# An encoder layer on one core: the score unit moves from the bias tables into the split factors of queries and keys, and four tiles are loaded at an earlier place in the code

## The chip, the core and the metric

The kernel runs on one core of a Trainium2 chip. A core has a matrix engine (TensorE, PE in the profile; PEld is its loading of weights), a vector engine (VectorE, DVE), a scalar engine (ScalarE, ACT), a general engine (GpSimd, POOL) and a queue engine (SyncE, SP), which in this kernel issues every DMA. Each engine runs its own list of instructions in order and waits on semaphores for the others. The metric is the device time of one execution in microseconds (us), lower is better.

## The reference

One layer of a bidirectional encoder with width 1024 is applied to two inputs with the same weights: a prompt of 512 positions and a sample of 1024 positions. The kernel treats them as three chunks of 512 positions: chunk 0 is the short sequence (the prompt), chunks 1 and 2 are the long one (the sample).

```python
def encoder_layer(x, ...):
    h = rmsnorm(x, n_pre)
    aq, ak, av, gq, gk, gv, gr, glr = split(h @ w_in)
    o_attn = dilated_attention(heads(aq), heads(ak), heads(av))   # 8 heads of 64
    o_gla = gla_mixer(gq, gk, gv, gr, glr, ...)                   # gated linear attention
    x = x + rmsnorm(concat([o_attn, o_gla]) @ w_out, n_post)
    h = rmsnorm(x, n_ffn_pre)
    a, g = split(h @ w_up)
    f = (gelu(dwconv_centred(a, conv_w, conv_b)) * g) @ w_down
    return x + rmsnorm(f, n_ffn_post)

# in each of the three branches of dilated_attention:
    s = einsum('bnqrhd,bnkrhd->bnrhqk', qb, kn) * (Dh ** -0.5)
    s = where(valid, s - slopes * dist, NEG)
```

The three branches (windows of 128, 512 and 2048 positions at strides 1, 4 and 16) are merged by their softmax denominators. The kernel computes them as one softmax: the penalties, the masks and how many branches see a key are in one table for each head, `nbias`, which is an input made on the host.

## The kernel before

**Numbers in two halves.** Every float32 operand of the large matrix products is split into a high and a low half of 16 bits (or of a shortened float32), and a product is three matmuls: high by high, high by low, low by high (`mm3`, lines 353 to 355). To use the range of 16 bits, each group of weight columns is scaled by a power of two that is measured on the chip. The class `Group` does that: `measure` squares the weights on ACT (L253), `finish` sums on PE (L260) and DVE (L261), makes the power on POOL (L367, L368) and DVE (L216), and stores in `undo` the factor that takes a product back to its true unit (L220, L265). The twelve blocks of 128 columns that hold queries and keys of both kinds of attention belong to six groups, `G_FM[0]` to `G_FM[5]`; the first four hold the attention's queries and keys, and each of these holds those of two heads.

**Queries and keys.** `store_fm` takes a finished projection block out of PSUM, splits it (`split_psum`: ACT L358 for the high half, DVE L363 for the low) and stores it in DRAM. Before the change queries are multiplied by the constant -2^-15 there and keys by 2^-15, whatever the group's scale, so that their products are in a unit of the group's own. That unit is kept in `Group.scores`: column 0 is the factor that turns a product into a true score (undo squared, over 8, times 2^30), column 1 its reciprocal.

**Attention.** `attention(seq)` goes through 8 heads, and in each through tiles of 128 queries: 8 tiles for the long sequence, 4 for the short. Tiles with more than 512 keys are done in two pieces, which makes 14 steps a head for the long sequence. A step's work is spread over the next eleven in a pipeline: `scores` (PE, L593 and L594, into a PSUM bank), `reduce` (DVE, L608: product times factor plus table, with a running minimum), `expo` (ACT, L620), `part_hi` (DVE L627 and POOL L628 for the reciprocal of the denominator, `rs`; ACT L631 for the high half of the probabilities `p`), `part_lo` (DVE, L638), `turn` (a transposing DMA from `p` to `pt`, L647), `pv` (PE, L674) and `out` (ACT, DVE, and a DMA to the mix in DRAM, L689). POOL also starts each tile with a copy of one column (L602).

The table of a head is `bias`: 128 rows by 1664 columns for the long sequence, 1152 for the short one. `load` brings it in (L559). Because the products are in the group's own unit, the table has to be brought to that unit too: it is multiplied on POOL by column 1 of `scores` in slices of 128 columns (L565), 13 slices a head for the long sequence and 9 for the short, 176 in all. The slices are queued in `tables`; those of the first two heads are done ahead of the pipeline, the others at up to two a step. Two heads' tables are held at a time: the table of head h+2 is loaded when head h has left its buffer.

**What runs beside what.** `_weave` alternates the steps of a main piece of work with those of a side piece. The long attention is woven into the input projection of chunks 1 and 2 (`main2`). Then `main3` (the projection of chunk 0 and half of the output projection of chunks 1 and 2, `outproj_early`) is woven with the linear attention of the long sequence. The rest of the output projection follows, then the MLP of chunks 1 and 2 with the short sequence's attention and linear attention beside it, and at last the MLP of chunk 0. `outproj_early` multiplies the first half of the mixed features (four tiles `mix`, loaded by `load_mix`, L961) by the output weights. The pool `early`, which holds these tiles, has four buffers for them.

**The order of the instructions.** The code is traced once, and a planner decides when the kernel is built in which order each engine and each queue gets its instructions. It goes by its own estimate of the times: among the instructions of an engine that are ready by that estimate it takes the one that the code has first. So the order on an engine is near that of the code but not the same, and a DMA can stand long before the place at which the code asks for it.

Of the kernel before, what the change touches and what calls it, by code (L numbers as in the profile page):

```python
# [7 lines left out]
F32 = mybir.dt.float32  # L8
# [5 lines left out]
ALU = mybir.AluOpType  # L14
# [156 lines left out]
def encoder(ctx, tc, xp, xs, n_pre, w_in, wg, g_gla, w_out, n_post, n_ffn_pre, w_up, conv, w_down,  # L171
# [51 lines left out]
    class Rows:  # L223
# [3 lines left out]
        def __init__(self, nm):  # L227
            self.scale = const.tile([128, 1], F32, name=f"rows_{nm}")
# [8 lines left out]
    class Group:  # L237
# [1 line left out]

        def __init__(self, nm, n, rows, *more, scores=False):
            self.n, self.rows, self.more, self.at = n, rows, more, 0

            self.scores = const.tile([128, 2], F32, name=f"scores_{nm}") if scores else None
            self.scale = const.tile([128, 1], F32, name=f"up_{nm}")
            self.undo = const.tile([128, 1 + len(more)], F32, name=f"undo_{nm}")

# [9 lines left out]
        def finish(self):  # L258
            ps, total = bank(), small()
            nc.tensor.matmul(ps[:, 0:self.n], ones, self.sums[:, 0:self.n], start=True, stop=True)  # L260
            nc.vector.tensor_reduce(out=total, in_=ps[:, 0:self.n], axis=mybir.AxisListType.X, op=ALU.add)  # L261
            power_of_two(self.scale, total, 1.0)
            u = self.undo[:, 0:1]
            times(u, self.scale, self.rows.scale)
            nc.vector.reciprocal(out=u, in_=u)  # L265
            for i, x in enumerate(self.more):
                if x is not None:
                    times(self.undo[:, 1 + i:2 + i], u, x)
            if self.scores is not None:
                c = [self.scores[:, i:i + 1] for i in range(2)]  # L270
                nc.gpsimd.tensor_scalar(out=c[0], in0=u, scalar1=u, scalar2=PART ** -2 / 8.0, op0=ALU.mult, op1=ALU.mult)
                nc.vector.reciprocal(out=c[1], in_=c[0])

    r_pre, r_fpre = Rows("pre"), Rows("fpre")

# [13 lines left out]
        + [O_GQ, O_GQ + 128, O_GK, O_GK + 128]  # L289
    FM_ORDER = [0, 4, 1, 5, 2, 6, 3, 7, 8, 9, 10, 11]  # L290
    TM = [(O_V, 256), (O_V + 256, 256), (O_GV, 256), (O_GV + 256, 256), (O_GR, 256), (O_GR + 256, 272)]
    G_FM = [Group(f"fm{i}", 4, r_pre, scores=i < 4) for i in range(6)]
    G_TM = [Group(f"tm{i}", 4, r_pre, (1.0 / PART / P_SCALE, None, 0.5)[i // 2]) for i in range(6)]
    G_UP = [Group(f"up{b}", 4, r_fpre, 0.5) for b in range(NFB)]
    GROUPS = [range(i, i + 3) for i in range(0, 18, 3)] + [range(18, 22)]
# [138 lines left out]
    def store_fm(c, i, ps):  # L434
        seq, o0 = where(c)
        m = FM_ORDER[i]
        if m < 8:
            t = tmp.tile([128, 2, CH], FP16, name="stq", tag="two")
            split_psum(ps, t[:, 0], t[:, 1], -PART if m < 4 else PART)
            nc.sync.dma_start(out=QK[seq][m][:, :, o0:o0 + CH].rearrange("s p t -> p s t"), in_=t)  # L440
            stored.add((c, m))
        else:
            o = stage.tile([128, CH], F32, name="sto", tag="sto", bufs=3)
            nc.scalar.activation(out=o, in_=ps, func=ACTF.Copy, scale=G_FM[i // 2].undo[:, 0:1])
            nc.sync.dma_start(out=GQK[seq][m - 8][:, o0:o0 + CH], in_=o)
# [99 lines left out]
    def attention(seq):  # L545
# [6 lines left out]
        with ExitStack() as es:  # L552
            hp = es.enter_context(tc.tile_pool(name=f"ah{seq}", bufs=nbuf, side="right", reuse_waits="tile"))
            up = es.enter_context(tc.tile_pool(name=f"au{seq}", bufs=2, side="right", reuse_waits="tile"))
            heads, vs, st, pts, pvs, tables = {}, {}, {}, {}, {}, []

            def load(h):
                bias = hp.tile([128, bw], F32, name="bias", tag="bias")
                nc.sync.dma_start(out=bias, in_=nbias[h, :, 0:bw])  # L559
                qs = hp.tile([128, T], FP16, name="qs", tag="qs")  # L560
                kk = hp.tile([128, 2, T], FP16, name="kk", tag="kk")
                unit = G_FM[h // 2].scores[:, 1:2]

                def scale(c0, c1):
                    nc.gpsimd.tensor_scalar(out=bias[:, c0:c1], in0=bias[:, c0:c1], scalar1=unit, scalar2=3e38,  # L565
                                            op0=ALU.mult, op1=ALU.min)
                tables.extend(lambda c0=c0: scale(c0, min(c0 + 128, bw)) for c0 in range(0, bw, 128))
                r = slice(h % 2 * DH, (h % 2 + 1) * DH)
                nc.sync.dma_start(out=qs, in_=QK[seq][h // 2][:, r, :])
                for s in range(2):  # L570
                    nc.sync.dma_start(out=kk[s * DH:(s + 1) * DH],
                                      in_=QK[seq][4 + h // 2][:, r, :].rearrange("s p t -> p s t"))
                heads[h] = (bias, qs, kk)
# [23 lines left out]
            def reduce(h, qt, k0, k1, last):  # L597
                bias = heads[h][0]
                miss = ph_sb[:, seq * 32 + h * nkt + qt:seq * 32 + h * nkt + qt + 1]
                if k0 == first[qt]:  # L600
                    st[h, qt] = up.tile([128, T + 1], F32, name="t", tag="t", bufs=1 + nh)
                    nc.gpsimd.tensor_copy(out=st[h, qt][:, T:T + 1], in_=miss)  # L602
                    st["m"] = miss
                t = st[h, qt]
                ps = st.pop((h, qt, k0))
                for a, b, col in bias_ranges(qt, k0, k1):
                    m = up.tile([128, 1], F32, name="m", tag="m", bufs=8)
                    nc.vector.tensor_tensor_reduce(  # L608
                        out=t[:, a:b], in0=ps[:, a - k0:b - k0], in1=bias[:, col:col + b - a],
                        scale=G_FM[h // 2].scores[:, 0:1],  # L610
                        scalar=st["m"], op0=ALU.add, op1=ALU.min, accum_out=m)
                    st["m"] = m
                if last:
                    st[h, qt] = (t, m)
# [84 lines left out]
            for h in range(nbuf):  # L699
                load(h)  # L700
                load_v(h)
                while tables:
                    tables.pop(0)()
            yield True
            stages = [(1, reduce, "piece"), (2, expo, "tile"), (3, part_hi, "tile"), (4, part_lo, "tile"),
                      (5, turn, "tile"), (9, pv, "pair"), (11, out, "pair")]
# [1 line left out]
            for i in range(len(steps) + 12):  # L708
                for lag, fn, kind in reversed(stages):
                    if not 0 <= i - lag < len(steps):  # L710
                        continue
                    x = steps[i - lag]
                    if kind == "piece":
                        fn(*x)
                    elif x[4] and kind == "tile":
                        fn(x[0], x[1])
                    elif x[4] and x[1] % 2:
                        fn(x[0], x[1] // 2)
                if i < len(steps):
                    scores(*steps[i])  # L720
                for _ in range(-(-bw // 128 * HEADS // len(steps)) + 1):
                    if tables:
                        tables.pop(0)()
                if i - 1 in ends:
                    h = ends[i - 1]
                    while not {(c, m) for c in cs for m in (h // 2, 4 + h // 2)} <= stored:
                        yield None
                    load(h)
                if i - 9 in ends:
                    load_v(ends[i - 9])  # L730
                yield True
# [225 lines left out]
    def load_mix(c, pool, bufs, ks=range(NK)):  # L957

        for k in ks:
            t = pool.tile([128, 2, CH], F32R, name="mix", tag="mix", bufs=bufs)  # L960
            nc.sync.dma_start(out=t.bitcast(F32), in_=MX[c][:, k * 128:(k + 1) * 128, :].rearrange("s p t -> p s t"))  # L961
            yield t
# [32 lines left out]
        for t in range(4):  # L995
            mm3(ps[t], tuple(m[:, s, t * 128:(t + 1) * 128] for s in range(2)), (wh[:, 0, :], wl[:, 0, :]), first, last)

    def outproj_early(c, pool):

        mix = list(load_mix(c, pool, 4, range(4)))  # L1000
        for half in range(2):
            ps = [bank(dense) for _ in range(4)]
            for k, m in enumerate(mix):
                outproj_step(ps, m, k == 0, k == 3)
                yield True
            for t in range(4):
                o = pool.tile([128, 512], F32, name="yp", tag="yp", bufs=2)
                nc.scalar.activation(out=o, in_=ps[t], func=ACTF.Copy)
                nc.sync.dma_start(out=rows(YP[c], t)[:, half * 512:(half + 1) * 512], in_=o)
# [150 lines left out]
    with ExitStack() as es:  # L1160
# [43 lines left out]
        def main3():  # L1204
            yield from inproj_fm([(0, h0[0])], range(12))
            yield from inproj_tm([(0, h0[0])], (4, 5))
            for c in (1, 2):
                yield from outproj_early(c, early)
        with tc.tile_pool(name="early", bufs=1, side="right", reuse_waits="tile") as early:
            _weave(main3(), linear(1), 46, 188)  # L1210
        act2 = ctx.enter_context(tc.tile_pool(name="act2", bufs=1, side="right", reuse_waits="tile"))
        mx = es.enter_context(tc.tile_pool(name="mx", bufs=1, side="right", reuse_waits="tile"))
# [129 lines left out]
```

## Time and profile before

| | us |
|---|---|
| median of 3 runs | 2166.89 (2157.13 to 2170.65) |
| the profiled execution, its own time | 2164.9 |
| its span | 2163.1 |
| mean granted PE clock, share of full speed | 0.94 |
| long attention beside the projection, about | 138 to 491 |
| linear attention of the long sequence, early output projection, about | 500 to 786 |
| short attention beside the MLP, about | 905 to 1170 |

All times in the profile are us from the span's start unless marked ns. In the slices of the page the span is cut into 40 equal parts of 54 us, and each digit is a busy share in tenths; the row PEclk is the clock that PE was granted. A line of a group names the source line, the engine, the operation, output and inputs with shapes, the count, and then busy time in us, the mean of one in ns, the idle time of the engine just before these instructions and what ended most of it. In a row of waits stand the engine, what it waited to do, what ended the wait, the total in us, how often, and the longest. In a timeline stand start, length, engine, line and instruction, and in brackets the idle time before it with what ended it; in the merged rows of a timeline, x13 is thirteen instructions of one kind.

### The profile page before, as it was taken

To read this page: it belongs to the slowest core of one execution; us is meant where nothing else is said; L and a number is where in the kernel's file an instruction comes from. 1 tells how busy PE (TensorE), PEld (TensorE's weight loads), DVE (VectorE), ACT (ScalarE), POOL (GpSimd) and SP (SyncE) were. 2 spreads that over 40 slices of the span, in tenths; PEclk is the share of its full clock that TensorE was granted. 3 is DMA by queue.
4 is the path that set the end of the run, shared out by engine and by line. 5 is a ranking of instruction groups with operands and counts; after the bars stand their busy time and mean duration, and the time that the engine had idled before them with its cause. 6 is when DMAs were issued, how large, how long until landed. Compare 5 with 4: busy or idle time off the path is not lost. (4 is left out here: it accounts for less than half of the span.)

```text
span 2163.1 us, 31915 instructions
## 1 busy us (share of the span) xinstructions
PE 1914.6 (89%) x11960; PEld 1199.5 (55%) x11960; DVE 1203.2 (56%) x2383; ACT 974.8 (45%) x1858; POOL 355.9 (16%) x697
## 2 busy tenths in 40 slices
PE   3797776888888958898898999999999998999997
PEld 3664334665457737744545564656564774565554
DVE  4256544575544426756466555465555378566666
ACT  5256545565524214645655453343333264433343
POOL 3303243331011002343321000010100031000001
PEclk8898887899999879999899999999999999999998
DMA  6468988987534466844544131222140466333331
GB/s 199 114 137 181 160 169 152 157 168 213 176 114 153 157 230 213 245 99 105 124 99 95 45 98 59 59 77 70 40 156 25 150 229 209 107 103 102 93 103 49
DMA packets 393118, 283.14 MB, mean 131 GB/s; under 512 B 174306, under 2 KB 342498, under 8 KB 392964
## 3 DMA queue, kind: packets, MB, share of 16 engines
q1 hardware_dynamic: 392964, 281.11, 48.2%
q8 instruction: 94, 1.54, 0.3%
q14 instruction: 60, 0.49, 0.1%
HBM read 196.02 MB, written 51.48 MB: 114 GB/s over the span
## 5 line engine op out<-in xcount | busy, mean ns | idle before, releaser
L353 PE MATMUL bank<-c,w_hi 128*128 128x512 f16 x704 | 267.0, 379 | 0.0
L354 PE MATMUL bank<-c,w_hi 128*128 128x512 f16 x704 | 266.8, 379 | 0.0
L355 PE MATMUL bank<-c,w_lo 128*128 128x512 f16 x704 | 266.8, 379 | 0.0
L353 PEld LDWEIGHTS <-w_hi 128*128 128x128 f16 x1376 | 138.3, 100 | 167.9 <-issue 21.9
L355 PEld LDWEIGHTS <-w_lo 128*128 128x128 f16 x1376 | 136.8, 99 | 166.8 <-issue 9.4
L354 PEld LDWEIGHTS <-w_hi 128*128 128x128 f16 x1376 | 137.4, 100 | 151.1 <-issue 8.5
L111 ACT ACTIVATE w_hi<-w_raw,up_up 128x512 f16<-128x512 f32 x176 | 125.8, 718 | 188.6 <-PE bank L354 101.3
L120 DVE SCALAR_TENSOR_TENSOR w_lo<-w_raw,up_up,w_hi 128x512 f16<-128x512 f32 x176 | 131.1, 747 | 98.1 <-PE bank L355 42.8
L111 ACT ACTIVATE w_hi<-w_raw 128x512 fp32r<-128x512 f32 x144 | 90.5, 629 | 209.4 <-PE bank L355 172.5
L353 PE MATMUL bank<-b,w_hi 128*128 128x512 f16 (+1 forms) x464 | 175.0, 378 | 6.4 <-DVE ya L1065 6.4
L355 PE MATMUL bank<-b,w_lo 128*128 128x512 f16 (+1 forms) x464 | 174.8, 377 | 5.1 <-DVE w_lo L120 5.1
L354 PE MATMUL bank<-b,w_hi 128*128 128x512 f16 (+1 forms) x464 | 175.0, 377 | 1.1 <-DVE b L363 1.1
L638 DVE SCALAR_TENSOR_TENSOR p<-t,rs,p 128x512 f16<-128x512 f32 (+2 forms) x96 | 89.9, 942 | 146.3 <-ACT p L631 145.6
L353 PE MATMUL bank<-w_hi,fh 128*128 128x512 f32 x352 | 143.1, 411 | 17.9 <-DVE ya L1099 13.9
L118 DVE TENSOR_TENSOR w_lo<-w_raw,w_hi 128x512 fp32r<-128x512 f32 x144 | 98.6, 689 | 99.2 <-PE bank L354 75.5
L1065 DVE SCALAR_TENSOR_TENSOR ya<-bank,cvt,ya 128x511 f32<-128x511 f32 x176 | 107.4, 614 | 62.5 <-ACT ya L1067 58.6
L354 PE MATMUL bank<-w_lo,fh 128*128 128x512 f32 x352 | 139.6, 397 | 0.8 <-DVE w_lo L118 0.8
L355 PE MATMUL bank<-w_hi,fl 128*128 128x512 f32 x352 | 139.6, 397 | 0.0
L631 ACT ACTIVATE p<-t,rs 128x512 f16<-128x512 f32 (+2 forms) x96 | 81.6, 859 | 127.0 <-POOL rs L628 117.1
L565 POOL TENSOR_SCALAR bias<-bias,scores_fm 128x128 f32<-128x128 f32 x176 | 127.7, 749 | 65.5 <-DMA bias<-in_nbias_dram 65.2
L253 ACT ACTIVATE w_junk<-w_raw 128x512 bf16<-128x512 f32 (+1 forms) x136 | 85.4, 628 | 114.6 <-DMA w_raw<-in_w_up_dram 69.8
L1135 DVE TENSOR_TENSOR y<-bank,y 128x512 f32<-128x512 f32 x144 | 97.4, 687 | 55.9 <-PE bank L355 55.3
(193 smaller groups left out, 4048.2 us busy)
## 6 DMA issues: line engine op xcount, KB each, us to landing
w_raw<-in_w_up_dram SPq DMA_DIRECT2D x88, 512.0 KB
w_raw<-in_w_in_dram SPq DMA_DIRECT2D x44, 512.0 KB
w_raw<-in_w_down_dram SPq DMA_DIRECT2D x36, 512.0 KB
mix<-mx SPq DMA_DIRECT2D x24, 512.0 KB
xin<-x SPq DMA_DIRECT2D x20, 512.0 KB
xin<-in_x_sample_dram SPq DMA_DIRECT2D x16, 512.0 KB
w_raw<-in_w_out_dram SPq DMA_DIRECT2D x32, 256.0 KB
bias<-in_nbias_dram SPq DMA_DIRECT2D x8, 832.0 KB
```

The costliest lines, as they stand in the source:

```text
L111: self.nc.scalar.activation(out=self.hi[i], in_=raw, func=ACTF.Copy, scale=1.0 if group is None else group.scale)
L118: self.nc.vector.tensor_tensor(out=lo, in0=raw, in1=hi.bitcast(F32), op=ALU.subtract)
L120: self.nc.vector.scalar_tensor_tensor(out=lo, in0=raw, scalar=group.scale, in1=hi, op0=ALU.mult, op1=ALU.subtract)
L253: nc.scalar.activation(out=junk[:, :raw.shape[1]], in_=raw, func=ACTF.Square, accum_out=self.sums[:, self.at:self.at + 1])
L353: nc.tensor.matmul(out, ah, bh, start=start, stop=False)
L354: nc.tensor.matmul(out, ah, bl, start=False, stop=False)
L355: nc.tensor.matmul(out, al, bh, start=False, stop=stop)
L565: nc.gpsimd.tensor_scalar(out=bias[:, c0:c1], in0=bias[:, c0:c1], scalar1=unit, scalar2=3e38, op0=ALU.mult, op1=ALU.min)
L631: nc.scalar.activation(out=p[:, 0:n], in_=t[:, kf:T], func=ACTF.Copy, scale=rs)
L638: nc.vector.scalar_tensor_tensor(out=p[:, n:2 * n], in0=t[:, kf:T], scalar=rs, in1=p[:, 0:n], op0=ALU.mult, op1=ALU.subtract)
L1065: nc.vector.scalar_tensor_tensor(out=out, in0=src, scalar=cw[:, j:j + 1], in1=out, op0=ALU.mult, op1=ALU.add)
L1135: nc.vector.tensor_tensor(out=y[t][:, cols], in0=ps[t], in1=y[t][:, cols], op=ALU.add)
```

## The change

The unit of the products goes into the factors with which queries and keys are split. With u the group's `undo` and P = 2^-15, keys are multiplied by min(u, P) and queries by -max(u / P, 1) u / 8. The product of the two is -u^2 / 8 in either case, so that the products of the score matmuls are true scores with the sign turned, and the table is used as it was loaded. `Group.heads` holds the two factors, made on POOL in `finish`; the queue of slices and its places in `attention` are gone, and the reduction multiplies by 1.0.

```diff
-            if self.scores is not None:
-                c = [self.scores[:, i:i + 1] for i in range(2)]
-                nc.gpsimd.tensor_scalar(out=c[0], in0=u, scalar1=u, scalar2=PART ** -2 / 8.0, op0=ALU.mult, op1=ALU.mult)
-                nc.vector.reciprocal(out=c[1], in_=c[0])
+            if self.heads is not None:
+                k, q = (self.heads[:, i:i + 1] for i in range(2))
+                nc.gpsimd.tensor_scalar(out=k, in0=u, scalar1=PART, scalar2=None, op0=ALU.min)
+                nc.gpsimd.tensor_scalar(out=q, in0=u, scalar1=1.0 / PART, scalar2=1.0, op0=ALU.mult, op1=ALU.max)
+                nc.gpsimd.tensor_scalar(out=q, in0=q, scalar1=u, scalar2=-0.125, op0=ALU.mult, op1=ALU.mult)
...
             t = tmp.tile([128, 2, CH], FP16, name="stq", tag="two")
-            split_psum(ps, t[:, 0], t[:, 1], -PART if m < 4 else PART)
+            f = G_FM[i // 2].heads
+            split_psum(ps, t[:, 0], t[:, 1], f[:, 1:2] if m < 4 else f[:, 0:1])
...
                 kk = hp.tile([128, 2, T], FP16, name="kk", tag="kk")
-                unit = G_FM[h // 2].scores[:, 1:2]
-
-                def scale(c0, c1):
-                    nc.gpsimd.tensor_scalar(out=bias[:, c0:c1], in0=bias[:, c0:c1], scalar1=unit, scalar2=3e38,
-                                            op0=ALU.mult, op1=ALU.min)
-                tables.extend(lambda c0=c0: scale(c0, min(c0 + 128, bw)) for c0 in range(0, bw, 128))
...
-                        out=t[:, a:b], in0=ps[:, a - k0:b - k0], in1=bias[:, col:col + b - a],
-                        scale=G_FM[h // 2].scores[:, 0:1],
+                        out=t[:, a:b], in0=ps[:, a - k0:b - k0], in1=bias[:, col:col + b - a], scale=1.0,
...
                 load_v(h)
-                while tables:
-                    tables.pop(0)()
...
                     scores(*steps[i])
-                for _ in range(-(-bw // 128 * HEADS // len(steps)) + 1):
-                    if tables:
-                        tables.pop(0)()
```

The second part moves the loading of the four `mix` tiles of chunk 1 from the start of its early output projection to a place ahead of `main3` and of the linear attention. The tiles of chunk 2 are loaded where they were.

```diff
-    def outproj_early(c, pool):
-
-        mix = list(load_mix(c, pool, 4, range(4)))
+    def outproj_early(c, pool, mix):
+
...
-            for c in (1, 2):
-                yield from outproj_early(c, early)
+            yield from outproj_early(1, early, mix)
+            yield from outproj_early(2, early, list(load_mix(2, early, 4, range(4))))
         with tc.tile_pool(name="early", bufs=1, side="right", reuse_waits="tile") as early:
+            mix = list(load_mix(1, early, 4, range(4)))
             _weave(main3(), linear(1), 46, 188)
```

More of the change, by code (lines that the diff above doesn't have):

```diff
@@ L237, in encoder, with __init__ @@
     class Group:
-        def __init__(self, nm, n, rows, *more, scores=False):
+        def __init__(self, nm, n, rows, *more, heads=False):
             self.n, self.rows, self.more, self.at = n, rows, more, 0
-            self.scores = const.tile([128, 2], F32, name=f"scores_{nm}") if scores else None
+            self.heads = const.tile([128, 2], F32, name=f"heads_{nm}") if heads else None
             self.scale = const.tile([128, 1], F32, name=f"up_{nm}")
@@ L291, in encoder @@
     TM = [(O_V, 256), (O_V + 256, 256), (O_GV, 256), (O_GV + 256, 256), (O_GR, 256), (O_GR + 256, 272)]
-    G_FM = [Group(f"fm{i}", 4, r_pre, scores=i < 4) for i in range(6)]
+    G_FM = [Group(f"fm{i}", 4, r_pre, heads=i < 4) for i in range(6)]
     G_TM = [Group(f"tm{i}", 4, r_pre, (1.0 / PART / P_SCALE, None, 0.5)[i // 2]) for i in range(6)]
@@ L554, in attention @@
             up = es.enter_context(tc.tile_pool(name=f"au{seq}", bufs=2, side="right", reuse_waits="tile"))
-            heads, vs, st, pts, pvs, tables = {}, {}, {}, {}, {}, []
+            heads, vs, st, pts, pvs = {}, {}, {}, {}, {}
             def load(h):
```

## The prediction, before the result was known

> **What bounds the kernel now.** I read the page first: busy shares, then the 40 slices.
>
> ```profile
> span 2163.1 us, 31915 instructions
> PE 1914.6 (89%) x11960; PEld 1199.5 (55%) x11960; DVE 1203.2 (56%) x2383; ACT 974.8 (45%) x1858; POOL 355.9 (16%) x697
> PE   3797776888888958898898999999999998999997
> PEclk8898887899999879999899999999999999999998
> L565 POOL TENSOR_SCALAR bias<-bias,scores_fm 128x128 f32<-128x128 f32 x176 | 127.7, 749 | 65.5 <-DMA bias<-in_nbias_dram 65.2
> ```
>
> TensorE (PE) is the bound: the second half of the slices is nearly full at full clock. What can be gained lies in the first half, where both the busy share and the granted clock (PEclk) are low. POOL is busy only 16%, but a third of that is the scaling that the change removes, and its 65.2 us of waiting for the table's DMA stand on an engine that runs in order. So the next view was who waits for whom, from 138 to 500 us, where the long sequence's attention runs beside its input projection.
>
> ```profile
> PE bank L593 <- DVE m L608: 48.4, 16, 9.7
> PE bank L674 <- issue: 18.1, 4, 6.1
> DVE p L638 <- ACT p L631: 106.5, 37, 15.1
> ACT p L631 <- POOL rs L628: 93.7, 29, 15.1
> POOL bias L565 <- DMA bias<-in_nbias_dram: 47.5, 6, 9.3
> ```
>
> Columns: total us, times, longest. Read upwards it is one chain: POOL waits for a table, ACT's p waits for POOL's rs, DVE's second half of p waits for ACT, and PE's score matmul (L593) waits for a PSUM bank that DVE's reduce (L608) frees. The timeline of the four engines and of SP around one of the six table loads shows it:
>
> ```profile
> 212.06 0.54 SPq L559 DMA_DIRECT2D bias<-in_nbias_dram  x1
> 213.59 0.64 POOL L602 COPY t<-ph_sb 128x1 f32<-128x1 f32 x1 [1.37 <-DVE p L638]
> 223.54 9.04 POOL L565 TENSOR_SCALAR bias<-bias,scores_fm 128x128 f32<-128x128 f32 x13 [9.31 <-DMA bias<-in_nbias_dram]
> 232.67 0.23 POOL L628 TENSOR_SCALAR rs<-rs 128x1 f32<-128x1 f32 x1
> 218.95 0.07 DVE L608 DVE_READ_ACCUMULATOR2_ANT m<- 128x1 f32 x1
> 232.93 1.15 ACT L631 ACTIVATE p<-t,rs 128x1024 f16<-128x1024 f32 x1 [15.14 <-POOL rs L628]
> 234.11 1.28 DVE L638 SCALAR_TENSOR_TENSOR p<-t,rs,p 128x1024 f16<-128x1024 f32 x1 [15.09 <-ACT p L631]
> 225.90 2.16 PE L674 MATMUL bank<-pt,v 128*128 128x256 f16 x12 [3.96 <-issue]
> 238.00 0.53 PE L593 MATMUL bank<-kk,qs 128*128 128x448 f16 x1 [3.49 <-DVE m L608]
> ```
>
> POOL does no other work from 214.2 to 232.67: 9.31 us of waiting and 13 slices in 9.04 us, about 18 us. The two small operations of the softmax (L628, L602) stand behind it, and DVE and ACT do nothing for 15 us. PE holds out on projection work for a while, then waits. Six heads have this; the last two, during which no further table is loaded, have none. Stage by stage:
>
> ```profile
> 142.00:423.00 281.00, 217.16 (x1225) 125.20 (x1223) 157.25 (x391) 152.74 (x280) 91.45 (x195) 0.86 0.86 165
> 423.00:491.00 68.00, 57.20 (x469) 46.27 (x468) 52.27 (x113) 48.30 (x83) 19.80 (x45) 0.94 0.77 161
> 461.00:491.00 30.00, 27.56 (x238) 22.80 (x237) 25.32 (x53) 21.70 (x37) 9.13 (x17) 1.00 0.83 172
> 237.00:249.00 12.00, 6.95 (x24) 3.34 (x24) 10.30 (x26) 9.58 (x20) 1.80 (x6) 0.50 0.91 189
> 408.00:424.00 16.00, 9.93 (x66) 7.10 (x65) 3.39 (x11) 1.28 (x3) 9.27 (x14) 0.80 1.13 137
> 905.00:1085.00 180.00, 156.36 (x760) 88.79 (x759) 98.52 (x230) 100.05 (x204) 75.21 (x140) 0.93 0.50 117
> 1085.00:1125.00 40.00, 40.00 (x207) 19.87 (x205) 24.52 (x57) 20.90 (x38) 12.09 (x24) 1.00 0.43 101
> ```
>
> Columns: stretch, length, busy us of PE, PEld, DVE, ACT, POOL, then granted clock, DMA share and GB/s. I use busy PE times clock as the work done, in us at full clock. The row from 237 shows the second half of a stall's price: after it, PE ran 12 us at a clock of 0.50.
>
> **The change part by part.** The sum is made against the profiled execution: 2164.9 us, of which 2163.1 are span; that is 2.0 below the median of 2166.89.
>
> *The slices in the long attention (104, of which 78 lie inside six heads).* They go, with the wait in front. In the first row (heads 0 to 5 with the six blocks) PE did 217.16 x 0.86 = 187 us of work in 281. Without blocks the same work takes 187 over the share of the time that PE then works. From rows: the last two heads reach 57.20 x 0.94 / 68 = 0.79, but their first part still recovers from the block that ends at 423; the last head alone reaches 27.56 x 1.00 / 30 = 0.92, but it has no loads of tables, queries or keys beside it. At 0.79 the stretch takes 237 us (44 less), at 0.92 203 (78 less). I take the middle, 0.85: 220 us, **61 less**. What is late next: the vector engines, busy 157 us of these 281 on DVE, would be at 157/220 = 71%, which they bear (25.32 of 30 in the last head); and the DMA, a rival below. The table itself is now waited for by L608 on DVE, behind which DVE's weight splits and banks would queue; it is issued when the head two before has finished, so it has about one head (over 30 us) for the 11.5 us from 212.06 to 223.54. I count that wait at nothing; the rival prices it.
>
> *The slices in the short attention (72), beside the MLP.*
>
> ```profile
> ACT p L631 <- POOL rs L628: 23.4, 7, 9.5
> 955.75 6.29 POOL L565 TENSOR_SCALAR bias<-bias,scores_fm 128x128 f32<-128x128 f32 x9 [4.76 <-DMA bias<-in_nbias_dram]
> 968.52 0.58 PE L353 MATMUL bank<-b,w_hi 128*128 128x512 f16 x1 [4.47 <-DVE ya L1065]
> ```
>
> The first row is the wait from 905 to 1125. The block is shorter (11 us) and PE has more other work, but DVE's convolution (L1065) then comes late. From 905 to 1085 PE did 156.36 x 0.93 = 145 us in 180: 35 lost. Not all comes from the blocks (a group's end stalls too, when the down projection needs its last column blocks), and the block at 1101 lies in a stretch of 40 us without loss. Between 0 and 35 I take half, **17 less**.
>
> *The first 26 slices.*
>
> ```profile
> 58.27 3.48 POOL L565 TENSOR_SCALAR bias<-bias,scores_fm 128x128 f32<-128x128 f32 x5
> 62.71 1.28 DVE L408 SCALAR_TENSOR_TENSOR xin<-xin,small,g 128x1024 f32<-128x1024 f32 x1 [6.64 <-POOL small L368]
> 64.14 1.09 PE L415 MATMUL bank<-idt,xin 128*128 128x128 f32 x4 [6.67 <-DVE xin L408]
> ```
>
> They hold back the row scale of the last input tile, and with it DVE and PE, by up to 6.6 us. What follows there waits for weights from memory, so between 0 and 6.6 I take **3 less**.
>
> *The score unit.* Four groups lose one POOL operation and one reciprocal on DVE and get three POOL operations; each group's are done before its first store, some beside the norms:
>
> ```profile
> L271 POOL TENSOR_SCALAR scores_fm<-undo_fm x4: 265/266/267, 14.4 to 156.9; 128x1 f32<-128x1 f32 x4
> L358 ACT ACTIVATE stq<-bank x24: 573/578/658, 49.6 to 596.3; 128x512 f16<-128x512 f32 x24
> L358 ACT ACTIVATE a<-bank,rows_pre x16: 672/687/714, 18.1 to 522.7; 128x512 f16<-128x512 f32 x16
> L363 DVE SCALAR_TENSOR_TENSOR stq<-bank,stq x24: 672/688/693, 52.3 to 600.8; 128x512 f16<-128x512 f32 x24
> L363 DVE SCALAR_TENSOR_TENSOR a<-bank,rows_pre,a x16: 740/743/751, 21.2 to 523.4; 128x512 f16<-128x512 f32 x16
> ```
>
> Eight more on POOL at 0.27 us are 2.1 us, of which 0.5 stand ahead of the first norms: **1 more**, between 0 and 2. The 24 stores of queries and keys now take their factor from a tile. The nearest operation that does so (into a) costs 0.11 us more on ACT and 0.055 on DVE: 2.6 and 1.3 us, hidden beside PE's projection; with that cover gone, 4 us. The other way, 176 reductions (L608) take 1.0 instead of a tile's factor; by the same 0.055 DVE gains up to 9.7 us, or nothing. It isn't PE's time; I count nothing.
>
> *The mix tiles.* The order on each queue is made by a planner when the kernel is built, not by the code, and there the tiles are early already:
>
> ```profile
> 504.11 0.66 SPq L961 DMA_DIRECT2D mix<-mx  x1
> 517.44 1.52 SPq L961 DMA_DIRECT2D mix<-mx  x3
> L353 PE MATMUL bank<-w_hi,mix x192: 387/393/797, 690.6 to 1734.7; 128*128 128x512 f32 x192
> ```
>
> PE first reads them at 690.6, over 170 us after their issue. Moved up, they are the same four DMAs of about 0.5 us of SP, at most 2 us ahead of the gates' loads and a weight load, with PE still on projection work: nothing, between 0 and 2.
>
> Sum: 61 + 17 + 3 - 1 = 80 less: 2164.9 - 80 = **2085**.
>
> **The rivals.** *Full gain.* PE works at the last head's 0.92 through the long attention (78), nearly all the short one's loss goes (30) and the start gives 5: 113 less, 2052. For it: the vector engines have room. Against it: the last head has no loads beside it. One page speaks for it: the Trainium skill, "DMA: Bandwidth & Descriptors", Latency and other measured facts, puts a transposing DMA at 261 GB/s, so that DMA should not be what limits here; the trace's 137 GB/s from 408 to 424, where transposes share the queue with a table, does not reach that.
>
> *DMA becomes the bound.* DMA share times 281 us is 0.86 x 281 = 242; if the engines can't hold more than one, the stretch shrinks by 39 at most, and by 13 if no more than 0.9. For it: 1.13 at only 137 GB/s, and PE's value matmuls (L674) waiting 18.1 us with no compute engine late, just after transposes behind a table. Against it: a share over one means that packets' times include queueing. With 26 for the stretch, 10 for the short one and 3 at the start less 1: 38 less, 2127.
>
> *The wait moves to DVE, and the kernel is slower.* If the planner now issues a table late, DVE's reduce stops in order with everything behind it. Today a block costs POOL 18 us a head. A wait of the 8 us that POOL now waits (47.5/6) leaves some gain, about 2130. From 18 us a head on it turns to a loss; at 25 us, 6 x 7 = 42 more, 2207. Against it: the load's place in the code and the buffers that let it start are the same.
>
> *It does nothing for PE* (other work hides the blocks): 2165. Against it: the 48.4 us and the clock of 0.50.
>
> **How the numbers follow.** Forecast (2062 to 2110) 0.52; full gain 0.18; DMA 0.18; wait on DVE with some gain 0.05, with a loss 0.03; nothing 0.04. About 1% is what a measurement of this kernel can tell from no change. Faster by more (below 2145): 0.52 + 0.18 + 0.18 + 0.04 = 0.92, where the wait with some gain counts 0.04; within 1%: 0.05; slower: 0.03. The range takes in the forecast, the DMA case and most of the full gain: 2045 to 2132.
>
> **What would show it.** Right: no POOL line of 9 us in the attention, ACT's wait for rs below 20 us from over 90, heads of some 37 us where they took 47, a clock near 0.95 from 142 on, PE's bank waits on L608 below 20. Wrong: waits of DVE's L608 for the table's DMA, value matmuls waiting longer for their transposes, or a clock still at 0.86. The stretch from 1200 on should only shift. What would break the forecast most easily is another order of the queues: the planner sees different times on POOL and may place everything else anew.

## The result, and the profile after

| | before | after |
|---|---|---|
| median of the runs on the same chip, us | 2162.77 (2157.13 to 2170.65) | 2094.15 (2091.49 to 2099.08) |
| the profiled execution's span, us | 2163.1 | 2097.3 |
| mean granted PE clock | 0.94 | 0.954 |

The ratio is 0.9683, with a 95% interval from 0.9642 to 0.9723: 68.6 us less. The forecast was 2085 with a range of 2045 to 2132, so the time came out 9 us above the forecast and inside the range.

These lines of the page of after answer to the first fence of the prediction: span, busy shares, PE's slices and clock. The table's slices (L565) have no successor; the last line is now the group that computes the high half of `p`.

```profile
span 2097.3 us, 31743 instructions
PE 1898.3 (91%) x11960; PEld 1194.8 (57%) x11960; DVE 1194.5 (57%) x2379; ACT 976.5 (47%) x1858; POOL 235.4 (11%) x529
PE   3898888798999958999999999999999979999997
PEclk8998989998899979999999999999999989999998
L627 ACT ACTIVATE p<-t,rs 128x512 f16<-128x512 f32 (+2 forms) x96 | 81.4, 858 | 74.6 <-DMA pt<-p 54.6
```

POOL has 120 us less work. Line numbers have moved by three or four: scores are L590 and L591, reduce is L605, `rs` on POOL L624, `p` on ACT L627 and on DVE L634, the transposing DMA L643, the value matmuls L670. What the last line says is new: ACT, before it may write `p`, waits 54.6 us for old transposes (the DMA from `p` to `pt`) that still read the buffer.

To say where the time went, the stages need markers that exist in both kernels. The first and last `rs` on POOL serve; these rows give count, durations in ns, and first and last start, for the long sequence (x64) and the short one (x32), first of before, then of after.

```profile
L628 POOL TENSOR_SCALAR rs<-rs x64: 203/209/1171, 141.9 to 488.9; 128x1 f32<-128x1 f32 x64
L628 POOL TENSOR_SCALAR rs<-rs x32: 208/220/759, 930.7 to 1155.0; 128x1 f32<-128x1 f32 x32
```

```profile
L624 POOL TENSOR_SCALAR rs<-rs x64: 207/208/1302, 133.2 to 448.1; 128x1 f32<-128x1 f32 x64
L624 POOL TENSOR_SCALAR rs<-rs x32: 207/208/758, 890.5 to 1085.1; 128x1 f32<-128x1 f32 x32
```

| stage, us | before | after | difference | forecast |
|---|---|---|---|---|
| start to the first `rs` | 141.9 | 133.2 | -8.7 | -3, and 1 for the unit |
| long attention | 347.0 | 314.9 | -32.1 | -61 |
| from there to the short attention | 441.8 | 442.4 | +0.6 | 0 |
| short attention | 224.3 | 194.6 | -29.7 | -17 |
| from there to the end of the span | 1008.1 | 1012.2 | +4.1 | 0 |

Together that is 65.8 less, against a forecast of 80. The last row is spread between runs: the same kernel, run again (below), took 1004.5 there. So the sum came out near, but the two large terms did not: the long attention gave half of its forecast, the short one nearly twice.

The waits of after in the long attention (130 to 460 us), to be set beside those of before from 138 to 500:

```profile
PE bank L590 <- DVE m L605: 21.2, 10, 3.8
PE bank L670 <- issue: 16.2, 3, 6.8
PE bank L670 <- DMA pt<-p: 8.4, 3, 3.2
DVE p L634 <- ACT p L627: 78.7, 40, 9.3
ACT p L627 <- DMA pt<-p: 48.3, 7, 9.3
ACT p L627 <- POOL rs L624: 15.4, 18, 2.7
```

The old chain is gone: ACT's wait for `rs` fell from 93.7 us (longest 15.1) to 15.4 (longest 2.7), and POOL waits for no table. But DVE still waits 78.7 us for ACT's `p`, where it was 106.5, and the reason is the row above the last: ACT waits 48.3 us, seven times, for transposes. Before, that row, and the one of the value matmuls, were these:

```profile
ACT p L631 <- DMA pt<-p: 2.8, 1, 2.8
PE bank L674 <- DMA pt<-p: 2.6, 2, 2.2
```

The timeline of after shows one of the seven waits, first SP's queue and then the engines:

```profile
202.47 0.58 SPq L562 DMA_DIRECT2D bias<-in_nbias_dram  x1
203.10 0.58 SPq L568 DMA_DIRECT2D kk<-qk  x1
203.78 12.28 SPq L643 DMA_TRANSPOSE pt<-p  x3
216.15 0.54 SPq L92 DMA_DIRECT2D w_raw<-in_w_in_dram  x1
```

```profile
216.04 1.15 ACT L627 ACTIVATE p<-t,rs 128x1024 f16<-128x1024 f32 x1 [5.65 <-DMA pt<-p]
217.23 1.28 DVE L634 SCALAR_TENSOR_TENSOR p<-t,rs,p 128x1024 f16<-128x1024 f32 x1 [6.29 <-ACT p L627]
215.99 1.38 PE L670 MATMUL bank<-pt,v 128*128 128x256 f16 x12 [2.53 <-DMA pt<-p]
```

A table and the keys' second half are issued, and the three transposes behind them, those of the last three tiles of a head, keep SP for 12.28 us. `p` has three buffers; ACT wants the next, its old transpose has not read it, and DVE waits for ACT. PE's value matmuls wait for the same transposes. The table's load, which had delayed `rs` by way of POOL, is now one of the transfers ahead of them; how much of the delay is its own, the experiments have to show. Rows by stretch (length, busy us of PE, PEld, DVE, ACT and POOL, granted clock, DMA share, GB/s) put the two kernels side by side. First come the long and the short attention of before, then the long attention of after, its part up to the end of the sixth table's wait at 382 us (the prediction cut before at 423 us, likewise at the end of the sixth block), the rest of it, and its short attention:

```profile
142.00:489.00 347.00, 272.36 (x1675) 169.77 (x1673) 207.78 (x502) 199.44 (x360) 110.73 (x239) 0.87 0.85 164
931.00:1155.00 224.00, 200.41 (x937) 106.25 (x935) 134.27 (x315) 125.03 (x252) 70.51 (x140) 0.95 0.47 103
```

```profile
133.00:449.00 316.00, 267.23 (x1683) 168.85 (x1681) 202.57 (x502) 201.32 (x362) 58.82 (x163) 0.92 0.96 180
133.00:382.00 249.00, 208.08 (x1210) 120.97 (x1207) 153.03 (x391) 154.00 (x280) 37.52 (x120) 0.92 0.99 182
382.00:449.00 67.00, 59.15 (x473) 47.88 (x474) 49.55 (x111) 47.32 (x82) 21.30 (x43) 0.92 0.82 176
890.00:1085.00 195.00, 189.79 (x921) 102.82 (x920) 131.76 (x315) 125.35 (x253) 32.31 (x86) 0.99 0.51 115
```

In the long attention the DMA engines' share rose from 0.85 to 0.96, and to 0.99 up to 382 us. Share times length hardly changed: 0.85 x 347 = 295 us before, 0.96 x 316 = 303 after. In the short attention, at a share of 0.51, PE is now busy 189.79 of 195 us at a clock of 0.99, where it was 200.41 of 224 at 0.95.

### The profile page after: what moved, and what is told of

It reads as the page before. It is cut to its first block, busy times and chain, and to the rows that moved or that the text cites. A ratio compares the mean times of both kernels' runs of the same rounds, so it can differ in the third digit from the quotient of the medians.

```text
span 2097.3 us, 31743 instructions
## 1 busy us (share of the span) xinstructions
PE 1898.3 (91%) x11960; PEld 1194.8 (57%) x11960; DVE 1194.5 (57%) x2379; ACT 976.5 (47%) x1858; POOL 235.4 (11%) x529
## 5 line engine op out<-in xcount | busy, mean ns | idle before, releaser
L356 PE MATMUL bank<-b,w_hi 128*128 128x512 f16 (+1 forms) x464 | 172.4, 372 | 1.0 <-DVE b L365 1.0
L355 PE MATMUL bank<-b,w_hi 128*128 128x512 f16 (+1 forms) x464 | 172.5, 372 | 0.0
L634 DVE SCALAR_TENSOR_TENSOR p<-t,rs,p 128x512 f16<-128x512 f32 (+2 forms) x96 | 89.7, 943 | 94.6 <-ACT p L627 94.2
L254 ACT ACTIVATE w_junk<-w_raw 128x512 bf16<-128x512 f32 (+1 forms) x136 | 85.5, 628 | 121.2 <-DMA w_raw<-in_w_up_dram 74.8
L627 ACT ACTIVATE p<-t,rs 128x512 f16<-128x512 f32 (+2 forms) x96 | 81.4, 858 | 74.6 <-DMA pt<-p 54.6
L355 PE MATMUL bank<-w_hi,a 128*128 128x256 f16 (+1 forms) x384 | 108.9, 285 | 7.4 <-DVE v2t L365 6.7
```

The lines of the kernel that those rows point to most:

```text
L254: nc.scalar.activation(out=junk[:, :raw.shape[1]], in_=raw, func=ACTF.Square, accum_out=self.sums[:, self.at:self.at + 1])
L355: nc.tensor.matmul(out, ah, bh, start=start, stop=False)
L356: nc.tensor.matmul(out, ah, bl, start=False, stop=False)
L627: nc.scalar.activation(out=p[:, 0:n], in_=t[:, kf:T], func=ACTF.Copy, scale=rs)
L634: nc.vector.scalar_tensor_tensor(out=p[:, n:2 * n], in0=t[:, kf:T], scalar=rs, in1=p[:, 0:n], op0=ALU.mult, op1=ALU.subtract)
```

## The experiments

The theory after the result had two parts. First, the whole gain comes from POOL's slices, which no longer stand in front of `rs`; the moved tiles add nothing. Second, the long attention gave only half because the DMA engines became its limit. The rivals: that the load moved early contributes; that the wait for the table's DMA, not the slices' own time, was the cost; that something else (a buffer too few, the queue by which the table is issued) holds the long attention.

### One part of the change at a time

Before with one line taken out, so that the tables are used as they were loaded, in another unit than the products (the penalties in its result are wrong, the other work is the same); before with the moved tiles alone; and the change without the moved tiles.

```diff
-                tables.extend(lambda c0=c0: scale(c0, min(c0 + 128, bw)) for c0 in range(0, bw, 128))
```

> The kernel before, with the slices left out and nothing else changed: the tables are not brought to the unit of the products, so the attention is computed with wrong penalties. If the slices on POOL in front of the softmax's small operations are the whole cause, it gains what the change gained, 60 to 75 us (2088 to 2103). If the cheaper reduction (606 against 666 ns on DVE, 176 times, 10 us in all) or the new order of the stores carries a part, it gains only 40 to 55 us.

```diff
-    def outproj_early(c, pool):
+    def outproj_early(c, pool, mix):
...
-            for c in (1, 2):
-                yield from outproj_early(c, early)
+            yield from outproj_early(1, early, mix)
+            yield from outproj_early(2, early, list(load_mix(2, early, 4, range(4))))
...
+            mix = list(load_mix(1, early, 4, range(4)))
```

> The kernel before with only the four mix tiles loaded at the earlier place. By my theory nothing: within 4 us of before, since the tiles were issued 170 us ahead of their use already. By the rival (they free the queue of DMAs later on, or hold it up) 5 us or more either way.

For the third the same edit was taken back in the changed kernel.

> The change without its second part: the score unit in the split factors, the mix tiles loaded at the old place. By my theory the same as the whole change, 2094 within 5 us. By the rival, 5 us or more behind it.

| kernel | median, us | ratio to before, 95% interval |
|---|---|---|
| before without the slices | 2086.3 | 0.9648 [0.9624, 0.9673] |
| before with the moved tiles | 2162.12 | 0.9999 [0.998, 1.0019] |
| the change without the moved tiles | 2091.72 | 0.967 [0.9649, 0.9691] |

The slices, with the wait for their table, are the whole gain, and the moved tiles nothing. Taking the slices out costs a line and gives 76 us; the changed kernel, which also pays for the unit in the split factors, gives 71 without the moved tiles. The two intervals overlap, so the unit's own price, some 5 us at most by the medians, is not told from nothing. The new wait is there without any other edit; from the waits of before without the slices, 130 to 460 us:

```profile
ACT p L630 <- DMA pt<-p: 45.1, 7, 9.3
ACT p L630 <- POOL rs L627: 13.6, 22, 1.8
```

One rival is left: that the slices slow DVE down while both work in the same memory. The records show no sign of it. The 80 pieces of the reduction that aren't the first of their tile took 523/676/810 ns (min/median/max) in before, and 523/676/812 ns with the slices taken out.

### The slices kept, but not in front of `rs` while the table is on its way

Before, with the slices of the long sequence held back for five steps, so that the table has landed, and then done a step at a time; a small operation on DVE makes their factor, so that they can't be moved ahead of that step.

```diff
+            held, HOLD = [0], 5 if nh == 2 else 0
...
-                for _ in range(-(-bw // 128 * HEADS // len(steps)) + 1):
-                    if tables:
-                        tables.pop(0)()
+                held[0] -= 1
+                if tables and held[0] < 0:
+                    gate = up.tile([128, 1], F32, name="gate", tag="gate", bufs=4)
+                    nc.vector.tensor_scalar(out=gate, in0=st["m"], scalar1=0.0, scalar2=tables[0][0], op0=ALU.mult, op1=ALU.add)
+                    for _ in range(-(-bw // 128 * HEADS // len(steps)) + 1):
+                        if tables:
+                            tables.pop(0)[1](gate)
```

> The kernel before with all 176 slices, but those of a later head held back: in the long attention they start five steps after the table was asked for, in the short one with the next step, up to two (four) a step, and each step's slices wait for that step's reduction through a small DVE operation. POOL does the same work but no longer waits for a table with the small operations behind it. If the in-order wait on POOL is the cause, most of the gain is there: 2095 to 2120. If POOL's work itself or its use of memory beside DVE is the cause, it stays near before, 2145 to 2170.

Measured: 2136.2, ratio 0.9879 [0.9856, 0.9901], 26 us less than before on that chip and short of what was expected. Its waits from 130 to 460 us:

```profile
ACT p L633 <- POOL rs L630: 46.5, 35, 3.8
ACT p L633 <- DMA pt<-p: 40.4, 6, 9.1
POOL bias L566 <- DVE gate L726: 17.7, 14, 2.5
```

The longest wait for `rs` fell from 15.1 to 3.8 us, so the table is no longer waited for; but 46.5 us are left in 35 pieces, and the transposes are waited for as in the changed kernel. So with the table's wait gone, a third of what leaving the slices out gives is there. Slices of 0.7 us still stand in front of an `rs` of 0.2 us, but the experiment also adds a wait of its own: in the last row POOL waits 17.7 us for the small operation on DVE, again with `rs` behind it. How much of the rest is the slices' own time stays open. By the markers, the long attention gained 11 us (336.1) and the short one, whose slices also came step by step, 18 (206.6).

### The long sequence alone

The change, with slices, unit and factor of the short sequence as they were before.

```diff
...
-            split_psum(ps, t[:, 0], t[:, 1], f[:, 1:2] if m < 4 else f[:, 0:1])
+            if seq:
+                split_psum(ps, t[:, 0], t[:, 1], f[:, 1:2] if m < 4 else f[:, 0:1])
+            else:
+                split_psum(ps, t[:, 0], t[:, 1], -PART if m < 4 else PART)
...
+                if not seq:
+                    tables.extend(lambda c0=c0: scale(c0, min(c0 + 128, bw)) for c0 in range(0, bw, 128))
...
+                        scale=1.0 if seq else G_FM[h // 2].scores[:, 0:1],
...
```

> The changed kernel, but with the short sequence as before: constant factors, tables brought to the products' unit by the 72 slices beside the MLP. The profiles of before and after put 29 us of the gain between the start of the short attention and its end, so by that reading this is 25 to 30 us slower than the changed kernel (2117 to 2124). By my prediction's sizes (61 long, 17 short) it is 17 slower, 2110.

Measured: 2125.83, ratio 0.9832 [0.9801, 0.9862]. Before stood at 2161.58 on this chip, so the long sequence and the start are worth 36 us, and the other 32 of the change's 68 are the short sequence's. Its short attention, by the same marker, is back at 223.5 us, where the changed kernel has 194.6:

```profile
L639 POOL TENSOR_SCALAR rs<-rs x32: 207/222/758, 887.7 to 1111.2; 128x1 f32<-128x1 f32 x32
```

### What limits the long attention now

Seven runs on the changed kernel. A fourth buffer for `p` (paid for with one buffer each of `sto` and `stg`, the staging tiles of the projection's stores); the tables issued by ACT; only the tables of heads 0 and 1 loaded, and used by the later heads too; only the high half of `p` transposed, and read twice by the value matmuls; the last two together; and the changed kernel itself, with the fourth buffer again beside it. The third, fourth and fifth leave transfers out but no work of PE, DVE or ACT.

```diff
...
-                p = up.tile([128, 2 * T], FP16, name="p", tag="p", bufs=3)
+                p = up.tile([128, 2 * T], FP16, name="p", tag="p", bufs=4)
...
```

> The changed kernel with four buffers instead of three for the probabilities p; the space comes from one buffer each of the two staging tiles of the projection's stores (2 instead of 3). In the changed kernel ACT waits 48 us for old transposes to leave p. If this wait is what holds the heads at 41 us, most of it goes and the kernel gains 10 to 25 us (2070 to 2084). If the transposes themselves are too slow behind the table's load, the wait moves on to PE's value matmuls and nothing is gained, 2090 to 2098.

```diff
-                nc.sync.dma_start(out=bias, in_=nbias[h, :, 0:bw])
+                nc.scalar.dma_start(out=bias, in_=nbias[h, :, 0:bw])
```

> The changed kernel with the tables' loads issued from ACT instead of SP, so that they stand in another queue than the transposes. If the transposes are late because they stand behind the table in one queue, ACT's wait for p falls below 20 us and the kernel gains 10 to 20 us. If both share the same DMA engines' time, nothing changes but 16 issues on ACT: 2090 to 2100.

```diff
-                bias = hp.tile([128, bw], F32, name="bias", tag="bias")
-                nc.sync.dma_start(out=bias, in_=nbias[h, :, 0:bw])
+                bias = heads[h - 2][0] if h >= 2 else hp.tile([128, bw], F32, name="bias", tag="bias")
+                if h < 2:
+                    nc.sync.dma_start(out=bias, in_=nbias[h, :, 0:bw])
```

> The changed kernel with only the first two heads' tables loaded in each sequence; the later heads use them again, so their penalties are wrong. 8.4 MB of loads less. If the table's load is what delays the transposes, ACT's wait for p nearly goes and the kernel gains 15 to 30 us (2065 to 2080). If the transposes are slow by themselves, it gains less than 8 us.

```diff
-                nc.sync.dma_start_transpose(out=pts[h, qt // 2][:, 0:2 * nb, o:o + 128],
-                                            in_=st.pop((h, qt))[:, 0:2 * nb * 128])
+                nc.sync.dma_start_transpose(out=pts[h, qt // 2][:, 0:nb, o:o + 128],
+                                            in_=st.pop((h, qt))[:, 0:nb * 128])
...
-                        nc.tensor.matmul(ps[:, :n], v[:, kt, :], turned(pt, qp, j, kt, n), start=i + j == 0,
+                        nc.tensor.matmul(ps[:, :n], v[:, kt, :], turned(pt, qp, 0, kt, n), start=i + j == 0,
```

> The changed kernel with only the high half of the probabilities transposed; the value matmuls read the high half twice, so the result loses its low half while PE's work stays the same. The transposes move half the bytes (12.8 MB less in the long attention). If DMA time is what now bounds the long attention, ACT's wait for p and PE's wait for pt nearly go and the kernel gains more than leaving out the tables did: 25 to 40 us (2055 to 2070). If the vector engines' chain bounds it, it gains less than 8 us.

> Both: half of the transposes and only the first two heads' tables loaded (wrong penalties, low halves left out). If DMA is the only thing that stands between the changed kernel and a long attention at 0.92 to 0.95 of PE's clocked time, both together add: 2045 to 2060. If another bound is reached with one of them, it is as fast as the half transposes alone.

> The changed kernel once more, as the reference on this chip: 2094 within 4 us.

> The changed kernel with four buffers for p once more, beside it: by the first run 5 us faster than the changed kernel; if that was between chips, the same.

The third column is ACT's wait for transposes from 130 to 460 us, the fourth the long attention by its first and last `rs`.

| kernel | median, us | ratio to before, 95% interval | wait, us | long, us |
|---|---|---|---|---|
| the change, again | 2092.32 | 0.9673 [0.9654, 0.9692] | 46.1 | 315.1 |
| four buffers of `p` | 2089.33 | 0.9662 [0.9634, 0.9689] | 13.2 | 310.6 |
| four buffers, again | 2094.47 | 0.9682 [0.9655, 0.9709] | 13.7 | 309.1 |
| tables issued by ACT | 2102.83 | 0.9726 [0.9698, 0.9753] | 46.3 | 320.1 |
| two tables only | 2074.91 | 0.9603 [0.957, 0.9637] | 29.7 | 301.2 |
| half the transposes | 2076.31 | 0.9589 [0.956, 0.9618] | 28.7 | 297.3 |
| both | 2064.14 | 0.9543 [0.9524, 0.9562] | 6.5 | 290.1 |

A fourth buffer takes most of the wait away and gains nothing that can be told: the long attention is some 5 us shorter, but beside the changed kernel on the same chip the whole is 2 us longer, within both intervals. Its waits say why. First the change again, then four buffers again, both from 130 to 460 us:

```profile
ACT p L627 <- DMA pt<-p: 46.1, 7, 8.9
ACT w_junk L254 <- DMA w_raw<-in_w_in_dram: 7.0, 4, 3.9
```

```profile
ACT w_junk L254 <- DMA w_raw<-in_w_in_dram: 29.3, 7, 8.1
ACT p L627 <- DMA pt<-p: 13.7, 4, 4.6
```

Much of the time that ACT no longer waits for transposes it waits for the projection's weights (L254 squares them), whose loads stand in SP's queue between the transposes. So the buffer was only the place where a late transfer was met. What the staging buffers that it took would be worth was not measured alone.

Fewer bytes do help: 832 KB less for each of six heads' tables shortens the long attention by 14 us, half the transposes by 18, and both by 25. Neither alone takes the wait away. With two tables only, the same three transposes as in the timeline above, now behind queries and keys alone, still hold SP for 10.22 us (12.28 in the change), and ACT waits 3.91 us (5.65):

```profile
199.40 10.22 SPq L644 DMA_TRANSPOSE pt<-p  x3
209.43 1.15 ACT L628 ACTIVATE p<-t,rs 128x1024 f16<-128x1024 f32 x1 [3.91 <-DMA pt<-p]
```

So the table is one part of what makes the transposes late, not the whole. Half the transposes brought the DMA share down to 0.75, but gained 16 us of the kernel's time, where 25 to 40 were expected if DMA time bounds the stage. So it isn't the only bound. The stretch of half the transposes, and that of both (it ends 3 us before the last `rs`), by the columns above:

```profile
133.00:433.00 300.00, 265.42 (x1699) 168.65 (x1698) 204.31 (x505) 201.15 (x364) 58.25 (x162) 0.94 0.75 149
```

```profile
133.00:420.00 287.00, 256.90 (x1649) 163.44 (x1648) 198.87 (x493) 197.92 (x354) 55.02 (x160) 0.95 0.71 135
```

With both, PE's work is 256.90 x 0.95 = 244 us in 287, a ratio of 0.85; the changed kernel has 267.23 x 0.92 = 246 in 316, or 0.78. The work is nearly the same; taking the transfers out made the difference. With the tables issued by ACT they have a queue of their own (q10), but the wait for transposes stays (46.3 us) and the kernel is about 10 us slower than the change run again, the intervals just apart; why it is slower was not followed up. The queues of its page, with packets, megabytes and share:

```profile
q1 hardware_dynamic: 390660, 269.58, 48.0%
q10 hardware_dynamic: 2304, 11.54, 1.9%
```

So the tables standing ahead of the transposes in one queue is not what delays them. This agrees with the Trainium skill, "DMA: Bandwidth & Descriptors", Issuing engines are not separate DMA queues: transfers started by different engines run on the same 16 DMA engines and interleave, and another issuer saves only issue time.

One thing stays open. Half the transposes also relieve SP: from 133 us on (to 449 in the change, to 433 with half) the rows of L643, with count and min/median/max of SP's time in ns, are

```profile
L643 SPq DMA_TRANSPOSE pt<-p x62: 1212/2003/8214, 136.0 to 443.6; - x62
```

```profile
L643 SPq DMA_TRANSPOSE pt<-p x64: 1200/1246/5271, 134.1 to 432.7; - x64
```

A transpose held SP for 1.2 us at least in both, and for up to 8.2 us with all the bytes, 5.3 with half of them. How much of the 18 us is SP's time and how much the DMA engines' was not separated. In the run with two tables SP still issues every transpose, at a median of 1.9 us, and only six loads of some 0.6 us fall away, so there the gain comes from the transfers. Of the versions that compute all of it, none is clearly faster than the change.

## Why the prediction came out right, and where it did not

*The cause* was named as it is: slices of 128 columns on POOL, with the wait for their table, ahead of `rs`, and by way of ACT and DVE ahead of PE. Without them ACT's wait for `rs` fell from 93.7 to 15.4 us, and the 9 us lines of POOL are gone. That the mix tiles count nothing was right too (0.9999).

*The long attention, 61 forecast, 32 measured, is the mis-sized term.* The step was the share of the time that PE works once the blocks are gone: 0.85, the middle of 0.79 and 0.92. The six heads with blocks were to take 220 us. They took 249, up to the end of the sixth wait, and PE's 208.08 x 0.92 = 191 us of work (187 was forecast) make 0.77, below both rows that the prediction took as bounds. These bounds came from the last two heads, where the DMA share was 0.77 and 0.83; the six heads had 0.86 already with the blocks, and shortening them pushed it to 0.99. The last two heads took 67 us, where it was 68: there no change was forecast, and there is next to none. So the mechanism of the rival "DMA becomes the bound" was at work in this stage, and the 32 us lie between the 13 and the 39 that the rival allowed, near its 26. With tables and half of the transposes taken out, PE's ratio over the whole long attention is 0.85, and it takes 290.1 us, 57 less than before. So 25 of the 29 us that were missing come back when transfers, and with them some of SP's time, are taken out. What holds the stage then was not followed.

*The short attention, 17 forecast, 30 measured.* The prediction halved a loss of 35 us because groups' ends and the block at 1101 might not be the slices' doing. Nearly all of it was: with the slices back in the short sequence alone, its 29 us are lost again (223.5), and without them PE is at 189.79 of 195 us, beside a DMA share of 0.51. *The start, 3 forecast, 9 measured:* the 26 slices delayed more than the one stall of 6.6 us that was quoted; with nothing but the slices taken out, the first `rs` stands at 131.7 us. Short attention and start came out 19 us better than forecast, the long attention 29 us worse. That the total lies only 9 us from the forecast is in part luck.

*The score unit.* The costs by instruction were sized well. ACT's and DVE's halves of queries and keys, and DVE's reduction with 1.0 for a factor:

```profile
L360 ACT ACTIVATE stq<-bank,heads_fm x24: 664/670/749, 51.1 to 555.2; 128x512 f16<-128x512 f32 x24
L365 DVE SCALAR_TENSOR_TENSOR stq<-bank,heads_fm,stq x24: 732/748/752, 53.2 to 559.8; 128x512 f16<-128x512 f32 x24
```

ACT pays 670 - 578 = 92 ns (0.11 us was forecast), DVE 748 - 688 = 60 ns (0.055). On the reduction DVE gains the same: the median of its 96 first pieces went from 666 to 606 ns, over 176 pieces 10.6 us, against "up to 9.7 us, or nothing". As forecast, none of it shows in the time.

*What would show it.* The 9 us lines are gone, and ACT's wait for `rs` is 15.4 (below 20): right. PE's waits for banks of DVE are 21.2 (below 20 was said): nearly. Heads take 249/6 = 41.5 us, not 37, and the clock is 0.92, not 0.95: these two missed, and go with the wait for transposes. Of the wrong signs, L605 never waits for a table, and the value matmuls wait little more than before (16.2 and 8.4 us, where it was 18.1 and 2.6). The prediction looked for late transposes only at the matmuls that read `pt`; they showed at the writer of `p`, which has to wait until the old one is read. That wait it did not name.

## What to carry to other kernels

An in-order engine that waits for a transfer must not have a small operation of a latency chain behind it: blocks of up to 18 us of waiting and scaling a head, on an engine that is 16% busy, cost this kernel 3%. Before counting what a stall's removal gives, multiply the stage's DMA share by its length: here 295 us of transfers stood below a stage of 347, and no version that kept all transfers came below 309. That product is a warning and not a floor: the share was over 1 in one stretch of before (1.13), so it counts some time in which packets only queue, and with half the transposes the product fell to 225 us while the stage fell only to 297. When a removed wait comes back elsewhere, look at writers that wait for their buffers as well as at readers that wait for data, and test with fewer bytes before adding buffers.

## What the hardware showed that was not expected

- A factor in a 128x1 tile in place of a constant costs 92 ns on ACT and 60 ns on DVE for each instruction on 128x512, and the same 60 ns come back where a tile's factor becomes 1.0. For ACT, the Trainium skill, "ScalarE: Activation LUTs", What ACT_TABLE_LOAD costs, states about 93 ns for each such operand, and the trace agrees.
- The DMA engines at a share of 0.96 moved 180 GB/s in this mix of transposes, tables and weights, and 182 at 0.99. Share times length, 295 and 303 us, stayed nearly the same while the stage shrank by 31 us.
- Four buffers in place of three moved 32 us of waiting from one line of ACT (46.1 to 13.7) to another (7.0 to 29.3, in part) and left the time of the whole where it was.
